# Computing the whole gate half of a gMLP layer by seven block products instead of two thirds of it, in a two-layer trunk on one core

## The chip, the cores and the metric

The program runs on one core of one Trainium2 chip. The metric is the device time of one execution in microseconds (us); lower is better.

## What is computed

The reference is a trunk of two layers on 512 tokens of width 1024, all in float32:

```python
for i in range(DEPTH):
    mod = cond @ ada_w[i] + ada_b[i]                       # six rows of 1024: the adaLN modulation
    sh1, sc1, g1, sh2, sc2, g2 = split(mod, 6)
    h = rms_norm(x, norm_mix[i]) * (1.0 + sc1) + sh1
    y = chunked_relpos_attention(h, ...) if i == 0 else chunked_spatial_gating(h, ...)
    x = x + g1 * y
    h = rms_norm(x, norm_ffn[i]) * (1.0 + sc2) + sh2
    x = x + g2 * (square(relu(h @ w1)) @ w2)               # hidden width 4096

def chunked_spatial_gating(h, w_in, v_gain, w_s, b_s, w_out):
    u, v = split(gelu(h @ w_in), 2)                        # w_in is 1024 x 6144: u and v have 3072 columns
    v = rms_norm(v, v_gain)                                # over all 3072 columns of a token
    vm = mix_positions(v, w_s masked, b_s)                 # windows of 128 tokens
    return (u * vm) @ w_out
```

The change concerns `h @ w_in` for the v half (the gate half) in layer 1: a product of 512 x 1024 by 1024 x 3072.

## The kernel before, in words

**Products.** TensorE (PE) gets float32 operands as pairs: `Split` (L481) makes a rounded high part with a ScalarE cast (L487) and a low part with a VectorE subtract (L488). Every product of two tiles is three matmuls, hi by hi, hi by lo and lo by hi (`mm3`, L92).

**Places.** All large tiles live in 49 places of 4 KB per partition, which `Slots` (L36) hands out from one queue in the order in which they were given back. Whoever takes a place waits for its last user.

**Seven block products.** `seven` (L615) multiplies a 512 x 1024 left operand by a 1024 x 1024 right operand as 2 x 2 blocks of 512, with seven block products in place of eight. Each is done in two half-steps of 256 rows, 12 matmuls each: 168 matmuls for two column blocks of 512. The sums of right operands are made in their places: `plus` is a VectorE add (L632), `grow` a load from HBM that adds to what lies there, issued on GpSimd's queue (L629), and L662 the same from one place to another. A `Step` has four parts: load, right (sums and split of the right operand), left (`prep`, sums and split of the left operand) and mult. `Run.tick` (L724) does a load 7 steps ahead of a mult, and the two splits 3 steps ahead. `Kept` (L561) holds the split left operands of the normed h of layer 1, numbered 0 to 6 by product, for all uses in that layer. Products 0 and 1 use blocks of h itself; product 2 uses the difference of its two lower blocks (token tiles 2 and 3), made by L538.

**The gate half.** Its 3072 columns are six blocks of 512. Block 0 is done plainly by `gate_tile` (four token tiles of 24 matmuls), block 1 plainly by `gate_steps` (four steps of 24 matmuls), and blocks 2 to 5 as two pairs by `seven` with `own=(5, 6)`: the sums for products 5 and 6 are VectorE adds. `Gate.put` collects the results: the first product that reaches a tile is copied from PSUM (L1461), the next is added (L1464), then Gelu (L1465) and the square with its sum (L1467) follow, and each finished pair of tiles is stored to HBM as `vd` (L1438) and loaded again in the mixing. The plain blocks take Gelu straight from PSUM (L1483, L1485).

**Where it starts.** The end of the feed-forward of layer 0 (`project_last`) finishes the residual x tile by tile; `norm.rows(t)` normalizes token tile t and `norm.cols(t)` transposes it (L368) and modulates it on the way out of PSUM (L371, eight ScalarE instructions). The last tile is transposed only after 48 matmuls of the gate half have been issued, so that its norm is hidden. In this region PE follows the written order; elsewhere the scheduler orders each engine.

**Background.** The adaLN rows are worked off piece by piece (`bg`): a load of 512 KB (L179) and a VectorE multiply-add (L194) each, from a queue of 90 that `keep[0]` holds back until later stages.

## Time and profile before

| | |
|---|---|
| median of 3 runs | 1392.52 us (1390.43 to 1395.06) |
| the profiled execution | 1389.62 us, of it 1387.8 us from the first to the last instruction |
| PE busy | 1365.1 us, 98% of the span |
| VectorE (DVE), ScalarE (ACT) busy | 985.6 us, 742.3 us |
| granted TensorE clock | 0.997 of full speed (mean) |

How to read it: the feed-forward of layer 0 runs from 367 us to about 640 us, the gate half from there to about 778 us, and mixing, output product and the second feed-forward follow. The other engines' busy time lies beside PE's unless PE waits; their idle time costs nothing by itself.

### The profile page before, as it was taken

What the parts mean: (1) busy time and instruction counts of PE and PEld (TensorE: products, weight loads), DVE (VectorE), ACT (ScalarE), POOL (GpSimd) and SP (SyncE); (2) the same over time, 40 slices, a digit from 0 to 9 for tenths busy, and PEclk for the clock granted to TensorE, in tenths of its full rate; (3) what the DMA queues carried; (4) which work ended last, traced back from release to release, by engine and by line L of the source; (5) the groups of instructions that cost most, each with busy time, mean ns of one, the idle gap of its engine ahead of it and who ended that gap; (6) DMA issues with size and microseconds to landing.
All of it is one profiled execution on the core that took longest, in us unless ns stands there. A gap on an engine that the chain in (4) does not pass through costs nothing.

```text
span 1387.8 us, 18908 instructions
## 1 busy us (share of the span) xinstructions
PE 1365.1 (98%) x7130; PEld 1168.0 (84%) x7130; DVE 985.6 (71%) x1430; ACT 742.3 (53%) x1249; POOL 83.5 (6%) x98
## 2 busy tenths in 40 slices
PE   8999999999999999999999999999999999999998
PEld 7899888789888888888888888888889988888887
DVE  6889999685657776677796786778855445665672
ACT  6537667665454545537576644466435454554530
POOL 0000000001101102000000001000000110100100
PEclk9999999999999999999999999999999999999999
DMA  9756576574667776458446748575447376655541
GB/s 372 244 138 211 157 209 174 175 286 125 160 187 178 183 226 122 137 183 309 132 165 198 211 152 243 157 193 196 136 136 244 76 155 194 136 155 134 107 152 61
DMA packets 97483, 246.68 MB, mean 178 GB/s; under 512 B 8680, under 2 KB 10096, under 8 KB 97392
## 3 DMA queue, kind: packets, MB, share of 16 engines
q1 hardware_dynamic: 79536, 205.62, 44.6%
q0 software_dynamic: 16128, 33.56, 14.6%
q10 hardware_dynamic: 1728, 6.29, 1.2%
q8 instruction: 56, 0.92, 0.3%
q14 instruction: 35, 0.29, 0.1%
HBM read 219.23 MB, written 14.68 MB: 169 GB/s over the span
## 4 chain that ended last, share of the span: by engine, by line
PE 86%; DVE 6%; DMA 4%; issue 2%; ACT 2%; SPq 0%; POOL 0%; DVEq 0%; ACTq 0%; POOLq 0%
PE p L92 83%; DMA s<-in_a_w_in 1%; DMA s<-xsg 1%; DMA s<-in_ada_w 1%; PE p L1633 1%; DVE s L1222 1%; DVE s L1265 0%; PE p L1260 0%; DMA s<-vd 0%; ACT s L487 0%; DMA s<-s 0%; PE p L207 0%; PE p L317 0%; DVE s L427 0%; DVE s L194 0%
## 5 line engine op out<-in xcount | busy, mean ns | idle before, releaser
L92 PE MATMUL p<-s,s 128*128 128x512 f32 (+2 forms) x6496 | 1302.5, 360 | 9.6 <-DVE nm L1222 2.9
L92 PEld LDWEIGHTS p<-s,s 128*128 128x128 f32 x6496 | 1094.4, 189 | 192.2 <-DVE nm L1222 4.6
L488 DVE TENSOR_TENSOR s<-s,s 128x1024 fp32r<-128x1024 f32 x308 | 371.0, 1223 | 217.6 <-ACT s L487 157.6
L487 ACT CAST s<-s 128x1024 fp32r<-128x1024 f32 x308 | 316.3, 1051 | 195.1 <-PE p L92 106.5
L769 ACT ACTIVATE r<-p 128x512 f32<-128x512 f32 x64 | 38.2, 597 | 123.1 <-PE p L92 121.4
L194 DVE SCALAR_TENSOR_TENSOR s<-s,cs,s 128x1024 f32<-128x1024 f32 x70 | 89.7, 1281 | 12.3 <-DMA s<-in_ada_w 11.7
L629 POOL DMA_DIRECT2D s<-in_ffn_w x48 | 58.3, 1215 | 496.0 <-DVE s L488 408.9
L525 DVE TENSOR_TENSOR s<-s,p 128x512 f32<-128x512 f32 x76 | 50.3, 683 | 15.5 <-PE p L92 15.2
L390 ACT CAST s<-s 128x1024 fp32r<-128x1024 f32 x36 | 37.4, 1051 | 37.8 <-DMA s<-in_ffn_w 14.9
L391 DVE TENSOR_TENSOR s<-s,s 128x1024 fp32r<-128x1024 f32 x36 | 43.4, 1222 | 10.3 <-ACT s L390 10.1
L775 ACT ACTIVATE s<-r 128x256 f32<-128x256 f32 (+1 forms) x112 | 44.9, 442 | 1.4
L426 DVE TENSOR_TENSOR tr<-p,s 128x512 f32<-128x512 f32 (+1 forms) x33 | 22.0, 672 | 31.6 <-PE p L92 31.3
L538 DVE TENSOR_TENSOR s<-s,s 128x1024 f32<-128x1024 f32 x28 | 33.6, 1223 | 10.9 <-PE p L92 10.5
L1227 ACT ACTIVATE s<-s,nm 128x128 f32<-128x128 f32 (+3 forms) x64 | 36.0, 564 | 7.8 <-DVE nm L1222 6.4
L632 DVE TENSOR_TENSOR s<-s,s 128x1024 f32<-128x1024 f32 x28 | 34.0, 1224 | 4.9 <-DMA s<-in_b_w_in 4.7
L321 ACT ACTIVATE tt<-p,mod,mod 128x128 f32<-128x128 f32 x64 | 24.0, 462 | 21.0 <-PE p L317 7.7
L427 DVE TENSOR_TENSOR s<-s,tr 128x512 f32<-128x512 f32 (+1 forms) x33 | 22.1, 675 | 15.0 <-DMA s<-xsg 14.4
L304 ACT ACTIVATE s<-s 128x512 f32<-128x512 f32 x24 | 15.3, 636 | 32.6 <-DVE s L427 30.3
L1265 DVE TENSOR_TENSOR s<-p,s 128x512 fp32r<-128x512 f32 (+3 forms) x64 | 29.3, 486 | 2.8 <-ACT s L1264 2.4
L1222 DVE CUSTOM_DVE_ANT_0 s<-p,s 128x128 f32<-128x128 f32 (+3 forms) x64 | 29.6, 486 | 1.9 <-PE p L92 1.7
L1637 ACT COPY s<-p 128x512 f32<-128x512 f32 x24 | 13.8, 583 | 26.8 <-PE p L1633 26.8
L1264 ACT CAST s<-p 128x512 fp32r<-128x512 f32 (+3 forms) x64 | 25.0, 427 | 5.5 <-PE p L1260 4.4
(149 smaller groups left out, 769.5 us busy)
## 6 DMA issues: line engine op xcount, KB each, us to landing
s<-in_ffn_w SPq DMA_DIRECT2D x116, 512.0 KB, 4.3
s<-in_ada_w SPq DMA_DIRECT2D x96, 512.0 KB, 5.4
s<-in_ffn_w POOLq DMA_DIRECT2D x48, 512.0 KB, 5.8
s<-in_b_w_in SPq DMA_DIRECT2D x48, 512.0 KB, 4.5
s<-in_b_w_out SPq DMA_DIRECT2D x24, 512.0 KB, 4.3
s<-in_a_w_in SPq DMA_DIRECT2D x22, 512.0 KB, 5.0
s<-s SPq DMA_DIRECT2D x64, 128.0 KB, 4.4
vd<-s ACTq DMA_DIRECT2D x12, 512.0 KB, 3.8
```

Source lines behind the costliest of these rows:

```text
L92: T.matmul(ps, lhsT, rhs, start=start, stop=stop, skip_group_check=more)
L194: V.scalar_tensor_tensor(acc, r, ck, acc, ALU.mult, ALU.add)
L390: A.copy(hi, raw)
L391: engs[len(ids) // 2 % len(engs)].tensor_tensor(lo, raw, f32(hi), ALU.subtract)
L487: A.copy(self.hi, raw)
L488: mark[0] = V.tensor_tensor(self.lo, raw, f32(self.hi), ALU.subtract)
L525: V.tensor_tensor(dst, dst, ps, op)
L629: G.dma_start(raw[name, s_][0], block(i, j, s_), accum_op=ALU.add)
L769: A.activation(r, ps, AF.Relu)
L775: A.activation(d, v, AF.Square)
L1222: V.tensor_tensor_reduce(out=pt[it], in0=ps[:, 0:n], in1=b["bias"][:, 512 - n:512], scale=-1.0, scalar=-NEG, op0=ALU.add, op1=ALU.min, acc ...
L1227: last_of["exp"] = A.activation(pt[it], pt[it], AF.Exp, bias=nm[:, it:it + 1], scale=-1.0, accum_out=sm[:, it:it + 1])
```

## The change

- The gate half has three pairs of blocks, and all three go by `seven`. `gate_tile`, `gate_steps`, `gate_end` and `gate_load` are gone. The plan runs the first two pairs interleaved: products 0 and 1 of the first pair, products 0 and 1 of the second, product 2 of both, and then the rest one after the other.
- `own` is now `()`: the right operands of products 5 and 6 are made by adding transfers on GpSimd's queue in place of VectorE adds. For the first two pairs `far` is set: the sum for product 2 is made by an adding load right after product 0's split, and its VectorE add is dropped.
- `Kept.first` makes left operands 0 and 1 (from tokens 0 to 255); `prep` makes the others, operand 6 among them, which was made early before.
- In place of the load for block 0, the first seven ticks (loads and splits) run in `project_last`; eight ticks with a mult (96 matmuls) follow, with `norm.cols(3)` and the preparation of left operand 2 in their middle.
- A tick does its left part before its right part.
- Places that a store gives back (`xs0`, `xsg`, `vd`) go to a queue of their own, `stored`, and are handed first to tiles that a load fills.
- The feed-forward of layer 0 does four background pieces where it did three (nine times), and 27 rather than 36 are held back.

The diff, most unchanged lines left out, with the removed plain functions cut:

```diff
@@ -36,17 +36,25 @@
         self.pool, self.prefix = pool, prefix
-        self.q = deque(range(n))
+        self.q = deque((0, i) for i in range(n))
+        self.stored = deque()
         self.n = 0
-    def get(self, shape, dtype):
-        i = self.q.popleft()
+    def get(self, shape, dtype, load=False):
+        q, s = self.q, self.stored
+        if s and (not q or s[0][0] + (0 if load else 16) < q[0][0]):
+            q = s
+        i = q.popleft()[1]
         self.n += 1
     def free(self, *ids):
-        self.q.extend(ids)
+        self.q.extend((self.n, i) for i in ids)
+    def free_stored(self, *ids):
+        self.stored.extend((self.n, i) for i in ids)
 @with_exitstack
...
@@ -561,17 +569,14 @@
     class Kept(Spent):
-        def half(self, i):
+        def first(self):
             for j in range(2):
-                self.op[((0, 1), ("r", 6))[i][j]] = Split(self.ab[i, j][0], [P, 4, 256])
-        def rows(self):
-            return plain({(0, 0): self.op[0], (0, 1): self.op[1], (1, 0): self.op.get("r"), (1, 1): self.op.get(6)})
+                self.op[j] = Split(self.ab[0, j][0], [P, 4, 256])
         def prep(self, m):
-            if m in self.op:
+            if m in self.op or m < 2:
                 return
                 2: (("x", (1, 0), (1, 1), ALU.subtract),),
@@ -579,8 +584,8 @@
                 5: (((0, 0), (0, 0), (1, 0), ALU.subtract),),
                 self.comb(*c)
-            self.op[m] = Split(self.ab[("x", "x", (0, 1), (0, 0))[m - 2]][0], [P, 4, 256])
-            self.spend(*((), ("x",), ((0, 1),), ((0, 0), (1, 0), (1, 1)))[m - 2])
+            self.op[m] = Split(self.ab[("x", "x", (0, 1), (0, 0), (1, 1))[m - 2]][0], [P, 4, 256])
+            self.spend(*((), ("x",), ((0, 1),), ((0, 0), (1, 0)), ((1, 1),))[m - 2])
             if d not in self.ab:
@@ -612,7 +617,8 @@
-    def seven(left, src, y, own=None):
+    def seven(left, src, y, own=None, far=False):
         raw, op, ps = {}, {}, {}
@@ -622,7 +628,7 @@
             return src[r0:r0 + 256, j * 512:j * 512 + 512].rearrange("(k p) n -> p k n", p=P)
         def load(name, i, j, s_):
-            raw[name, s_] = t, n = SL.get([P, 2, 512], F32)
+            raw[name, s_] = t, n = SL.get([P, 2, 512], F32, True)
             SP.dma_start(t, block(i, j, s_))
         def grow(i, j, name, s_):
@@ -644,7 +650,7 @@
                     grow(*add, name, s_)
             name = {0: "x", 1: "z", 2: "x", 4: "y", 3: "x", 5: "w", 6: "z"}[m]
-            if m == 2:
+            if m == 2 and not far:
                 plus("x", "w", s_)
                 plus(*{5: ("w", "y"), 6: ("z", "x")}[m], s_)
@@ -652,7 +658,9 @@
             late = m in (5, 6) and m not in own and waited[0] is not None
                 op[m, s_] = Split(raw[name, s_][0], [P, 2, 512])
-            if m == 2 and 5 not in own:
+            if m == 0 and far:
+                grow(0, 1, "x", s_)
+            elif m == 2 and 5 not in own:
                 grow(1, 1, "w", s_)
                 plus("x", "y", s_)
@@ -724,7 +732,7 @@
         def tick(self):
             self.i += 1
-            for j, part in ((i + self.ll + self.lp, "load"), (i + self.lp, "right"), (i + self.lp, "left"), (i, "mult")):
+            for j, part in ((i + self.ll + self.lp, "load"), (i + self.lp, "left"), (i + self.lp, "right"), (i, "mult")):
                 if 0 <= j < n:
@@ -846,7 +854,7 @@
             if hf == 0:
                     SP.dma_start(xs[t], xt[t])
-                    SL.free(xid[t])
+                    SL.free_stored(xid[t])
         any_order()
         up_done(1)
@@ -1436,10 +1444,10 @@
         A.dma_start(vd[cb, b], v.rearrange("p t n -> p (t n)"))
-        SL.free(i)
+        SL.free_stored(i)
...
@@ -1458,79 +1466,18 @@
             dst = vv[cb, t // 2][0][:, t % 2, :]
                 self.seen.add((t, hf))
-                A.copy(dst, ps)
+                waited[0] = A.copy(dst, ps)
                 return
             tt = tp.tile([P, 512], F32, tag="tt", name="vq")
-            A.activation(tt, dst, AF.Square, accum_out=vss[:, t, cb:cb + 1])
+            waited[0] = A.activation(tt, dst, AF.Square, accum_out=vss[:, t, cb:cb + 1])
             if t % 2:
-    def gate_tile(cb, t, w):
...
-    steps = gate_steps(1)
-    for p in (1, 2):
-        steps += seven(kept, b_w_in[0][:, SGH + p * 1024:SGH + (p + 1) * 1024], Gate(p), (5, 6))
+    pre = [seven(kept, b_w_in[0][:, SGH + p * 1024:SGH + (p + 1) * 1024], Gate(p), (), p < 2) for p in range(3)]
+    steps = pre[0][:4] + pre[1][:4] + pre[0][4:6] + pre[1][4:6] + pre[0][6:] + pre[1][6:] + pre[2]
     bsT = cp.tile([P, SGG], F32, name="bsT")
...
@@ -1712,7 +1658,7 @@
             for n in range(8)
-    steps[3].mult = then(steps[3].mult, mixing)
+    pre[0][-1].mult = then(pre[0][-1].mult, mixing)
     steps[-1].mult = then(steps[-1].mult, row_scales)
         ahead[0] = wload(b_w_out[0][2048:3072, 0:512], KD)
@@ -1740,28 +1686,26 @@
         norm.rows(t)
             with tc.issue_after(normed[0].ins):
-                kept.half(0)
-    lead[0], keep[0] = 2, 36
-    ffn(0, mid, gate_rows, norm.cols, lambda: gate_load(0), [3] * 9, 2, last_of["o"])
+                kept.first()
+    run = Run(steps, 4, 3)
+    lead[0], keep[0] = 2, 27
+    ffn(0, mid, gate_rows, norm.cols, lambda: [run.tick() for _ in range(7)], [4] * 9, 2, last_of["o"])
+    ahead.clear()
     close(0, 5)
         SP.dma_start(xs[t], xt[t])
-        SL.free(xid[t])
-    keep[0] = 27
-    ws = [ahead.pop("w")]
-    for t in range(2):
-        gate_tile(0, t, ws[0][0])
+        SL.free_stored(xid[t])
+    for i in range(4):
+        with tc.issue_after(normed[0].ins) if i > 1 else nullcontext():
+            run.tick()
     norm.cols(NT - 1)
-    kept.half(1)
-    run = Run(steps, 4, 3)
+    kept.prep(2)
     with tc.issue_after(normed[0].ins):
-        run.prime()
-    for t in range(2, NT):
-        gate_tile(0, t, ws[0][0])
+        for _ in range(4):
+            run.tick()
     any_order()
-    SL.free(*ws[0][1])
     keep[0] = 9
```

What the programs' instruction lists show: matmuls of 128x512 go from 4614 to 4590, ACT casts of 128x1024 from 370 to 375, ACT copies of 128x512 from 122 to 128, DVE operations of 128x1024 (two tensors) from 446 to 443 and of 128x512 from 254 to 260, and GpSimd's transfers from 64 to 80 (10 of the 16 more from HBM, 6 from place to place). The attention layer's order does not change.

DVE at the first norm (token tile 0), before; `p` is the last product of the feed-forward, L426 and L427 add its gated result to x, L130 to L137 make the row scale and L308 the normed tile:

```order
L391 TENSOR_TENSOR s17_681_6130<-s9_679_6127,s43_680_6129 128x1024 [waits DMAHW3_49,Activation_49]
L426 TENSOR_TENSOR tr_6192<-p7_284_6167,s26_435_4480 128x512 [waits PE_49]
L427 TENSOR_TENSOR s16_415_4341<-s16_415_4341,tr_6192 128x512 [waits DVE_49]
L130 TENSOR_SCALAR ra_6203<-ss_6200 128x1 [waits Activation_49]
L133 SCALAR_TENSOR_TENSOR ru_6205<-ry_6204,ra_6203 128x1 [waits Activation_49]
L137 SCALAR_TENSOR_TENSOR ru_6205<-ru_6205,ry_6204 128x1 [waits DVE_49]
L308 TENSOR_SCALAR s36_689_6199<-s16_415_4341,ru_6205 128x1024 [waits DVE_49]
```

And in the change (every line is eight higher):

```order
L496 TENSOR_TENSOR s28_695_6173<-s43_687_6157,s14_694_6172 128x1024 [waits DMAHW1_49,Activation_49]
L496 TENSOR_TENSOR s29_692_6166<-s12_686_6155,s42_691_6165 128x1024 [waits DMAHW2_49,Activation_49]
L434 TENSOR_TENSOR tr_6236<-p4_286_6211,s17_435_4480 128x512 [waits PE_49]
L435 TENSOR_TENSOR s11_417_4347<-s11_417_4347,tr_6236 128x512 [waits DVE_49]
L138 TENSOR_SCALAR ra_6247<-ss_6244 128x1 [waits Activation_49]
L496 TENSOR_TENSOR s0_698_6180<-s26_688_6159,s25_697_6179 128x1024 [waits DMAHW5_49,Activation_49]
L141 SCALAR_TENSOR_TENSOR ru_6249<-ry_6248,ra_6247 128x1 [waits Activation_49]
L145 SCALAR_TENSOR_TENSOR ru_6249<-ru_6249,ry_6248 128x1 [waits DVE_49]
L316 TENSOR_SCALAR s7_703_6243<-s11_417_4347,ru_6249 128x1024 [waits DVE_49]
```

Three subtracts of right operands of the gate half have come between the last product of tile 0 and its norm, two of them ahead of the add, one behind the mean; each waits for a cast, and those casts wait for loads. In the same way two subtracts and a multiply stand ahead of the norm of token tile 2, where before there were none.

ACT around the last modulation (`norm.cols(3)`: L371 before, L379 in the change), before; `s` are places, `p` banks of PSUM, `vd` the stored gate half, and a wait on DMAHW or DMASW is for a transfer of SP's or ACT's, or of GpSimd's queue:

```order
L1483 ACT_TABLE_LOAD
L1483 ACTIVATE s27_700_6494<-p5_297_6495 128x512 [waits PE_49]
L1485 ACTIVATE vq_6529,vss_3643<-s27_700_6494 128x512 [waits Activation_49]
L1483 ACTIVATE s27_700_6494<-p4_298_6531 128x512 [waits PE_49]
L1485 ACTIVATE vq_6560,vss_3643<-s27_700_6494 128x512 [waits Activation_49]
L1438 DMA vd_3642<-s27_700_6494 128x1024 [waits DMAHW5_49]
L371 ACTIVATE s42_687_6197<-p7_299_6563,mod10_5676,mod11_5101 128x128 [waits PE_49]
L371 ACTIVATE s42_687_6197<-p7_299_6563,mod10_5676,mod11_5101 128x128 x3
L371 ACTIVATE s6_688_6198<-p6_300_6572,mod10_5676,mod11_5101 128x128 [waits PE_49]
L371 ACTIVATE s6_688_6198<-p6_300_6572,mod10_5676,mod11_5101 128x128 x3
L487 CAST s7_735_6752<-s39_717_6603 128x1024 [waits DMAHW1_49,DVE_49]
L487 CAST s11_739_6785<-s5_720_6609 128x1024 [waits DMAHW4_49,DMAHW2_49,DVE_49]
```

In the change, from the last instruction of the modulation on:

```order
L495 CAST s0_742_6742<-s34_693_6170 128x1024 [waits DMASW7_49]
L495 CAST s35_749_6788<-s11_737_6694 128x1024 [waits DMAHW0_49,PE_49,Activation_49]
L1469 COPY s42_736_6685<-p0_305_6658 128x512 [waits PE_49]
L1473 ACT_TABLE_LOAD
L1473 ACTIVATE s20_720_6571<-s20_720_6571 128x512 [waits DVE_49]
L1469 COPY s42_736_6685<-p7_306_6665 128x512 [waits PE_49]
L1473 ACTIVATE s20_720_6571<-s20_720_6571 128x512 [waits DVE_49]
L1475 ACTIVATE vq_6615,vss_3643<-s20_720_6571 128x512 [waits Activation_49]
L1475 ACTIVATE vq_6625,vss_3643<-s20_720_6571 128x512 [waits Activation_49]
L1446 DMA vd_3642<-s20_720_6571 128x1024
L495 CAST s15_753_6812<-s12_686_6155 128x1024 [waits DVE_49,PE_49]
L495 CAST s18_728_6648<-s21_727_6646 128x1024 [waits DVE_49]
```

The Gelu tables (ACT_TABLE_LOAD) were loaded before the modulation and are now loaded behind it; between the modulation and the cast of left operand 2 (`s18_728`) stand eleven more instructions, of which the first waits for a transfer on GpSimd's queue. Its lo part is made by DVE behind that cast.

DVE behind the last norm, before; `cs` is the condition of the background pieces (L194):

```order
L488 TENSOR_TENSOR s18_707_6582<-s42_687_6197,s25_706_6581 128x1024 [waits Activation_49]
L488 TENSOR_TENSOR s10_732_6720<-s0_714_6597,s41_731_6719 128x1024 [waits DMAHW3_49,Activation_49]
L194 SCALAR_TENSOR_TENSOR s19_704_6526<-s37_725_6672,cs_79,s19_704_6526 128x1024 [waits DMAHW6_49,DVE_49]
L632 TENSOR_TENSOR s0_714_6597<-s0_714_6597,s48_730_6717 128x1024 [waits DVE_49]
L488 TENSOR_TENSOR s1_709_6586<-s6_688_6198,s35_708_6585 128x1024 [waits Activation_49]
L194 SCALAR_TENSOR_TENSOR s19_704_6526<-s31_729_6714,cs_79,s19_704_6526 128x1024 [waits DVE_49]
```

And in the change, up to the lo part of left operand 2 (`s9_729`); L1472 adds a product's result to the gate half, L638 is `plus`, L546 makes the difference for left operand 2:

```order
L1472 TENSOR_TENSOR s20_720_6571<-s20_720_6571,p4_301_6587 128x512 [waits PE_49]
L1472 TENSOR_TENSOR s20_720_6571<-s20_720_6571,p2_302_6594 128x512 [waits PE_49]
L638 TENSOR_TENSOR s12_686_6155<-s12_686_6155,s2_733_6672 128x1024 [waits DVE_49]
L638 TENSOR_TENSOR s43_687_6157<-s43_687_6157,s11_737_6694 128x1024 [waits DMAHW0_49,DVE_49]
L546 TENSOR_TENSOR s21_727_6646<-s46_701_6241,s39_702_6242 128x1024 [waits Activation_49]
L496 TENSOR_TENSOR s40_743_6743<-s34_693_6170,s0_742_6742 128x1024 [waits DMASW7_49,Activation_49]
L496 TENSOR_TENSOR s31_750_6789<-s11_737_6694,s35_749_6788 128x1024 [waits Activation_49]
L496 TENSOR_TENSOR s19_754_6813<-s12_686_6155,s15_753_6812 128x1024 [waits Activation_49]
L1472 TENSOR_TENSOR s42_736_6685<-s42_736_6685,p4_307_6701 128x512 [waits PE_49]
L496 TENSOR_TENSOR s9_729_6649<-s21_727_6646,s18_728_6648 128x1024 [waits Activation_49]
```

Seven subtracts stand between the last norm and the first of these rows. The background pieces that stood here are gone into the feed-forward; the adds of `Gate.put`, two sums of right operands and the difference for left operand 2 have come, and the lo part stands last. On GpSimd's queue eight adding loads (L635) come in between the feed-forward and the mixing, where there were none; the last, into `s34_693`, waits for the first subtract behind the last norm, and the first ACT row of the change above waits for it. On PE, 48 matmuls stand between the transposes of `norm.cols(3)` and the first use of left operand 2; its hi part is used alone for six matmuls, and the seventh needs the lo part.

## Rows read from the trace of the kernel before

**Rows 1.** The page's first part: busy time of each engine, its share of the span and its number of instructions; and the head of its chain of work that ended last, by engine.

```profile
PE 1365.1 (98%) x7130; PEld 1168.0 (84%) x7130; DVE 985.6 (71%) x1430; ACT 742.3 (53%) x1249; POOL 83.5 (6%) x98
...
PE 86%; DVE 6%; DMA 4%; issue 2%; ACT 2%; SPq 0%; POOL 0%; DVEq 0%; ACTq 0%; POOLq 0%
```

**Rows 2.** Busy time of each engine by stretch (us from the span's start), with instructions, then the granted clock, the busy share of the DMA engines and GB/s: the feed-forward of layer 0, its last product, the plain blocks of the gate half, its other blocks.

```profile
367.00:607.00 240.00, 240.00 (x1069) 198.93 (x1068) 162.15 (x163) 119.70 (x162) 22.86 (x19) 1.00 0.67 179
607.00:652.00 45.00, 45.00 (x214) 37.50 (x212) 30.44 (x45) 22.80 (x53) 0.00 (x0) 1.00 0.68 247
652.00:711.00 59.00, 59.00 (x269) 48.90 (x268) 49.68 (x47) 38.10 (x65) 0.61 (x2) 1.00 0.53 177
711.00:778.00 67.00, 67.00 (x298) 55.46 (x297) 47.56 (x47) 45.48 (x75) 4.17 (x4) 1.00 0.63 193
```

**Rows 3.** PE's timeline: start, length, line, operation and count. L368 are the transposes of `norm.cols`.

```profile
613.27 1.03 PE L368 MATMUL p<-ident,s 128*128 128x128 f32 x8
...
636.84 1.03 PE L368 MATMUL p<-ident,s 128*128 128x128 f32 x8
637.62 14.32 PE L92 MATMUL p<-s,s 128*128 128x512 f32 x62
651.78 1.03 PE L368 MATMUL p<-ident,s 128*128 128x128 f32 x8
652.57 32.47 PE L92 MATMUL p<-s,s 128*128 128x512 f32 x142
```

**Rows 4.** DVE's timeline at the norms of token tiles 0 and 2, in the same form; in brackets idle time and what ended it.

```profile
609.77 0.21 DVE L130 TENSOR_SCALAR ra<-ss 128x1 f32<-128x1 f32 x1 [0.79 <-ACT s L304]
...
610.70 0.75 DVE L308 TENSOR_SCALAR s<-s,ru 128x1024 f32<-128x1024 f32 x1
...
631.22 0.22 DVE L130 TENSOR_SCALAR ra<-ss 128x1 f32<-128x1 f32 x1 [0.93 <-ACT s L304]
...
632.15 0.76 DVE L308 TENSOR_SCALAR s<-s,ru 128x1024 f32<-128x1024 f32 x1
```

**Rows 5.** ACT's timeline at a cast of the plain blocks' right operand and around the last norm, in the same form; in brackets idle time and what ended it.

```profile
603.76 1.05 ACT L390 CAST s<-s 128x1024 fp32r<-128x1024 f32 x1 [5.08 <-DMA s<-in_b_w_in]
...
647.78 1.28 ACT L1483 ACT_TABLE_LOAD   x1
649.07 0.60 ACT L1483 ACTIVATE s<-p 128x512 f32<-128x512 f32 x1
649.70 0.63 ACT L1485 ACTIVATE vq<-s 128x512 f32<-128x512 f32 x1
...
652.78 2.89 ACT L371 ACTIVATE s<-p,mod,mod 128x128 f32<-128x128 f32 x8
655.52 5.83 ACT L487 CAST s<-s 128x1024 fp32r<-128x1024 f32 x6
672.15 0.60 ACT L1483 ACTIVATE s<-p 128x512 f32<-128x512 f32 x1 [10.80 <-PE p L92]
```

**Rows 6.** DVE's timeline there: L308 is the last norm.

```profile
648.24 0.75 DVE L308 TENSOR_SCALAR s<-s,ru 128x1024 f32<-128x1024 f32 x1
648.91 3.49 DVE L488 TENSOR_TENSOR s<-s,s 128x1024 fp32r<-128x1024 f32 x3
652.32 3.92 DVE L194 SCALAR_TENSOR_TENSOR s<-s,cs,s 128x1024 f32<-128x1024 f32 x3
```

**Rows 7.** Groups of instructions by line and shape, of DVE from 367 to 1010 us and of ACT from 560 to 780 us: count, busy us and mean ns of one, idle time before them and what ended it.

```profile
L632 DVE TENSOR_TENSOR s<-s,s 128x1024 f32<-128x1024 f32 x28 | 34.0, 1224 | 4.9 <-DMA s<-in_b_w_in 4.7
L538 DVE TENSOR_TENSOR s<-s,s 128x1024 f32<-128x1024 f32 x12 | 14.4, 1222 | 4.8 <-PE p L92 4.8
L1464 DVE TENSOR_TENSOR s<-s,p 128x512 f32<-128x512 f32 x12 | 8.1, 686 | 1.7 <-PE p L92 1.7
...
L1461 ACT COPY s<-p 128x512 f32<-128x512 f32 x12 | 6.9, 586 | 2.4 <-PE p L92 1.6 <-DMA vd<-s 0.7
```

**Rows 8.** The page's part on DMA issues: out<-in, issuing queue and count, KB each, median us from issue to landing; the third row is of 607 to 660 us alone.

```profile
s<-in_ffn_w POOLq DMA_DIRECT2D x48, 512.0 KB, 5.8
s<-in_b_w_in POOLq DMA_DIRECT2D x6, 512.0 KB, 8.5
s<-in_b_w_in SPq DMA_DIRECT2D x11, 512.0 KB, 8.2
vd<-s ACTq DMA_DIRECT2D x12, 512.0 KB, 3.8
```

**Rows 9.** All adding loads from HBM (L629): the least, median and greatest time from issue to landing; GpSimd's timeline with two of them in the gate half; then rows of SP's timeline, two loads of the gate half's weights and a store of x.

```profile
DMA to landing us min/median/max: 5.6/6.0/10.4
...
754.77 1.21 POOL L629 DMA_DIRECT2D s<-in_b_w_in  x1 [71.98 <-DMA s<-in_b_w_in]
757.55 1.20 POOL L629 DMA_DIRECT2D s<-in_b_w_in  x1 [1.58 <-DVE s L632]
...
599.05 0.94 SPq L387 DMA_DIRECT2D s<-in_b_w_in  x2
...
630.32 0.33 SPq L1750 DMA_DIRECT2D xsg<-s  x1
```

**Rows 10.** The page's DMA queues: packets, MB, and the time of the packets as a share of 16 engines' span.

```profile
q1 hardware_dynamic: 79536, 205.62, 44.6%
q0 software_dynamic: 16128, 33.56, 14.6%
```

More of the change, by code (lines that the diff above doesn't have):

```diff
@@ L130, in rsqrt_m2 @@
             V.tensor_scalar(a, ss, ss2, EPS, ALU.add, ALU.add)
-        A.activation(y, a, AF.Abs_reciprocal_sqrt)
+        rooted[0] = A.activation(y, a, AF.Abs_reciprocal_sqrt)
         if w == 1:
@@ L155, in raw_tile @@
     def raw_tile(shape):
-        t, i = SL.get(shape, F32)
+        t, i = SL.get(shape, F32, True)
         return t, lambda: SL.free(i)
@@ L295, in split_of @@
         return [(tiles[k // 2][0][:, k % 2, :], tiles[k // 2][1][:, k % 2, :]) for k in range(2 * len(tiles))]
-    normed, squared = [None], [None]
+    normed, squared, rooted = [None], [None], [None]
     def norm_rows(t, eng=V):
@@ L1466, in put @@
             tt = tp.tile([P, 512], F32, tag="tt", name="vq")
-            A.activation(tt, dst, AF.Square, accum_out=vss[:, t, cb:cb + 1])
+            waited[0] = A.activation(tt, dst, AF.Square, accum_out=vss[:, t, cb:cb + 1])
             if t % 2:
                 v_store(cb, t // 2)
-    def gate_tile(cb, t, w):
-        if (cb, t // 2) not in vv:
-            vv[cb, t // 2] = SL.get([P, 2, 512], F32)
-        ps, pi = bank()
-        gemm_tok(kept.rows(), w, t, ps)
-        bg(1)
-        gate_end(cb, t, ps)
-        PS.free(pi)
@@ L1559, in mixing @@
         PS.free(pi)
-        kept.op.pop("r").free()
     def row_scales():
@@ L1675, in load @@
             hf, j, o = n // 4, 1 - n // 2 % 2, n % 2
-            t, i = raw[n] = SL.get([P, 2, 512], F32)
+            t, i = raw[n] = SL.get([P, 2, 512], F32, True)
             r0 = p * 1024 + j * 512 + o * 256
```

46 lines of the change are left out of this document (2 added, 44 removed).

## The prediction

> **What bounds the kernel now.** I read the page's busy times first: PE is busy 98% of the span and carries 86% of the chain that ended last [rows 1]. Then the stretches: from 367 to 778 us PE has no idle time that shows, with DVE at 68% to 84% of the time and ACT at 50% to 68%, and the full clock [rows 2]. So a matmul that goes away is worth its whole length, and anything else counts only where PE has to wait for it. Then I read PE's timeline for the pace and for the moments at which PE needs something [rows 3], and DVE's and ACT's for how long before those moments it was ready [rows 4 to 6]. The reader is to see there three places: the transposes of token tile 0 at 613.27 us, those of tile 2 at 636.84, and the first matmuls that use tokens 256 to 511, 48 matmuls behind the transposes of tile 3 at 651.78.
>
> A measurement of this kernel can tell about 0.3% from no change, 4.2 us.
>
> **The gain.** Two plain blocks are 2 x 96 = 192 matmuls, a pair by seven products is 168, so 24 go. 62 matmuls took 14.16 us from 637.62 to 651.78 [rows 3], 0.228 us each, so **-5.5 us**. That is all there is to win: PE had hardly any idle time in this stretch.
>
> **The first use of left operand 2.** Before, what stands 48 matmuls behind the transposes of tile 3 needs a cast of the modulated block, and ACT had it done in time and was then idle for 10.80 us [rows 5]. Now it needs the difference of two blocks, its cast and its subtract, behind work that has come in on both engines. PE wants the hi part at 652.57 + 48 x 0.228 = 663.5 us, and, six matmuls later, the lo part at 664.9.
>
> By DVE: the last norm begins at 648.24 and the next instruction at 648.91 [rows 6]. From there the change has seven subtracts at 3.49 / 3 = 1.16 us (657.1), two adds of a product at 0.69 (658.4), two sums at 1.22 (660.9), the difference at 1.22 (662.1), three more subtracts at 1.22 (665.8), an add (666.5) and the lo part (667.7) [rows 6, 7]. That is 2.8 us late.
>
> By ACT: the modulation ends at 655.52 [rows 5], and the first cast then waits for the last adding load. That load is issued when the first subtract has ended, at 650.1; the 48 in the feed-forward, where the DMA engines are as busy as here (0.67 and 0.68 [rows 2]), took 5.8 us in the median [rows 8], so it lands at 655.9. Two casts at 0.97 (657.9), a copy that waits for 24 matmuls, until 658.1 (658.7), the tables at 1.28 (660.0), Gelu, copy, Gelu at 0.6 (661.8), two squares at 0.63 (663.0) and two casts (665.0) [rows 5, 7]; then DVE's third subtract, which needs the first of these casts, the add and the lo part at 667.1, 2.2 us late.
>
> I take **+2.5 us**, between the two, since the DVE route hangs on where the last norm ends. The ends: 0, if DVE and ACT come to this place 2.8 us earlier than before; and with an adding load of 8.5 us [rows 8] or of 10.4, the slowest one [rows 9], 4.9 or 6.8 late.
>
> ACT's table load took 1.28 us and the next instruction began 1.29 us after its start, at 649.07 [rows 5]; no drain shows. The Trainium skill (ScalarE: Activation LUTs, "What ACT_TABLE_LOAD costs") counts 2.66 us for a switch, 1.38 of it a drain. By that the ACT route would end 1.4 us later and the sum would come out about 0.8 us higher; the trace of this kernel speaks for the shorter time.
>
> **The first norms.** Three subtracts come in ahead of the norm of tile 0. Before, it was ready at 610.70 + 0.75 = 611.45, 1.8 us before its transposes [rows 3, 4]. The subtract between mean and scale and the cast that it waits for cost about 1.4 of this; the other two are hidden if their loads have landed. That leaves 0.4 us. For tile 2 two subtracts and a multiply, 2 x 1.22 + 0.69 = 3.1 us, come ahead of a norm that was ready at 632.91, 3.9 us early: 0.8 is left. Nothing is lost at either if each row holds to 0.4 us. But the loads are those whose counterpart made ACT wait 5.08 us before [rows 5], and they are issued behind each other: at the 8.2 us that such a load took in the busy stretch [rows 8] in place of 4.7 (issued at 599.05 [rows 9], cast at 603.76), tile 0 would be 3.5 - 0.4 = 3.1 us late. I take **+0.5 us**, nearer the lower end, since the DMA engines are idle for a third of that time [rows 2]; ends 0 and 3.1.
>
> **What costs nothing.** Nine background pieces move into the feed-forward: a DVE instruction of 3.92 / 3 = 1.31 us each [rows 6], 11.8 us in 240 us where DVE is idle for 78 [rows 2]; without that cover they would cost at most these 11.8. Five casts at 0.97, six copies and six adds at 0.59 and 0.69, less three adds at 1.22 [rows 5, 7], are 8.4 us on ACT and 0.5 on DVE, beside a PE that has 126 us of work there while ACT is idle for 42 [rows 2]. Sixteen more transfers on GpSimd's queue: 64 took 14.6% of the span, 3.17 us each [rows 10], 51 us more. From 607 to 778 the DMA engines were busy 0.68 x 45 + 0.53 x 59 + 0.63 x 67 = 104 us of 171 [rows 2]; with 51 more it is 0.90, and less what the nine background loads took, which leave (44.6% of the span for 205.62 MB, so 1.6 us each [rows 10]), 0.82. Not full, but loads will land later. Where places go to loads behind a store, the load waits for the store: 3.8 us for `vd` [rows 8], within a lead of seven steps, 84 x 0.228 = 19 us. From the mixing on PE's order is the old one, and I count nothing.
>
> **The sum.** -5.5 + 2.5 + 0.5 = -2.5 us. The profiled execution took 1389.62 us, so it would take 1387.1; the median of the runs is 2.9 above that execution, so I forecast **1390.0 us**.
>
> **The rivals.**
>
> A, operand 2 is ready in time: the full gain, 1392.5 - 5.5 = **1387.0 us**, faster. For it: DVE stood idle 0.93 and 0.79 us at the norms [rows 4], and a last norm 2.8 us earlier is enough. Against it: the seven subtracts all stand behind that norm, whatever is ready earlier.
>
> B, slower: the adding loads do not overlap. Eight now stand on a queue that was empty here. If each begins only when the one ahead has landed, then the five last ones, which cannot begin before their base loads (issued behind the store at 630.32 [rows 9], landed about 636, an estimate from 4.7 and queuing) end at 636 + 5 x 5.8 = 665.0 in place of 655.9. ACT's first cast waits 9 us, operand 2 comes 11.1 us late, and the sum is -5.5 + 11.1 + 0.5 = +6.1, **1398.6 us**. From 4.5 us a load upwards it takes the whole gain. Against it: two adding loads were issued at 754.77 and 757.55 [rows 9], 2.8 us apart, and such loads took 5.6 us at the least [rows 9]; GpSimd did not wait for the first to land before it issued the second. The Trainium skill (DMA: Bandwidth & Descriptors, "Anatomy of one DMA — SWDGE (gpsimd) path") fits 2.0 us and the bytes over 436 KB per us to such a transfer, 3.2 us for 512 KB; by that B would end near 652 and cost nothing. The 5.8 us of the trace are against that figure.
>
> C, a norm waits for loads: tile 0 or tile 2 is late by the upper end, -5.5 + 2.5 + 3.1 = +0.1, **1392.6 us**, no change. For it: covers of 0.4 and 0.8 us, and DMA busier than before.
>
> That the change would not do what it says is no rival: the matmuls are counted.
>
> **How the numbers follow.** The forecast 0.48, A 0.25, C 0.17, B 0.10. Faster by over 0.3% (under 1388.3): nearly all of A and the low edge of the forecast, 0.27. Slower (over 1396.7): B less its milder part, and the worst of C, 0.10. Within: 0.63. The range goes from A less the spread of medians, 1386.2, to C with operand 2 at its 4.9, 1395.0; it leaves out B and the tails, about 0.15.
>
> **What would show it.** Right: 24 matmuls of 128x512 fewer; PE idle for 2 to 3 us near 664 us, with the subtract or the cast of operand 2 as releaser; the transposes at 613, 637 and 652 us within 1 us of their places; the distance from there to the mixing 3 us shorter. For A, no idle time of PE at 664. For B, a wait of several us of ACT for an adding load ahead of the tables. For C, PE idle ahead of a group of transposes. The prediction is wrong at its root if PE is idle by more than 1 us elsewhere between 660 and 780, which the cover of seven steps is to prevent, or if the feed-forward is longer, which nine background pieces would then have caused.

## The result: slower by 0.41%, 5.5 us of matmuls saved and 11 us of waits and slow clock added

The changed kernel took 1398.13 us in the median of 6 runs (1395.63 to 1399.69), the kernel before 1391.55 in 6 runs on the same chip: **ratio 1.0041, 95% interval 1.0028 to 1.0055** (it is not the quotient of the two medians, which is 1.0047 and lies inside the interval). The forecast was 1390.0 with a range to 1395.0 and 0.10 for slower. The profiled execution of the change took 1395.63 us, 1393.9 of it from the first to the last instruction, 6.1 more than before.

The head of its page, with the chain of work that ended last by engine; it answers to [rows 1].

```profile
PE 1363.0 (98%) x7106; PEld 1165.2 (84%) x7106; DVE 985.7 (71%) x1433; ACT 750.1 (54%) x1260; POOL 100.7 (7%) x114
...
PE 83%; DMA 6%; DVE 5%; ACT 3%; issue 2%; SPq 0%; POOL 0%; DVEq 0%; POOLq 0%; ACTq 0%
```

PE has 24 instructions fewer, as counted, but its part of the chain fell from 86% to 83%, and that of DMA rose from 4% to 6%. The stretches of [rows 2], in the same columns, and a last one of 3.9 us:

```profile
367.00:607.00 240.00, 240.00 (x1068) 198.75 (x1068) 167.82 (x169) 117.22 (x160) 23.15 (x20) 1.00 0.70 192
607.00:652.00 45.00, 44.15 (x207) 36.31 (x206) 30.03 (x45) 26.45 (x56) 7.54 (x7) 1.00 0.81 227
652.00:711.00 59.00, 52.63 (x233) 43.21 (x232) 43.52 (x42) 40.09 (x65) 6.42 (x8) 0.94 0.69 178
711.00:778.00 67.00, 67.00 (x296) 54.94 (x295) 45.48 (x46) 47.23 (x78) 8.40 (x8) 1.00 0.85 235
672.10:676.00 3.90, 3.90 (x10) 3.12 (x11) 3.90 (x6) 3.49 (x7) 0.00 (x0) 0.53 0.00 0
```

The feed-forward is as it was, PE without idle time. The loss sits between 652 and 711 us: 6.4 us idle, and a granted clock of 0.94. PE's timeline there, which answers to [rows 3], and its transposes in the second feed-forward (L325):

```profile
615.47 1.06 PE L376 MATMUL p<-ident,s 128*128 128x128 f32 x8 [0.85 <-DVE s L316]
...
653.79 1.03 PE L376 MATMUL p<-ident,s 128*128 128x128 f32 x8
654.58 11.14 PE L100 MATMUL p<-s,s 128*128 128x512 f32 x48
672.09 27.64 PE L100 MATMUL p<-s,s 128*128 128x512 f32 x113 [6.37 <-ACT s L495]
...
1035.50 1.06 PE L325 MATMUL p<-ident,s 128*128 128x128 f32 x8 [1.21 <-DVE s L316]
1048.44 1.06 PE L325 MATMUL p<-ident,s 128*128 128x128 f32 x8 [0.94 <-DVE s L316]
1064.97 1.06 PE L325 MATMUL p<-ident,s 128*128 128x128 f32 x8 [1.19 <-DVE s L316]
```

The transposes of the second feed-forward that waited in the kernel before (L317 there):

```profile
1043.14 1.06 PE L317 MATMUL p<-ident,s 128*128 128x128 f32 x8 [0.59 <-DVE s L308]
1058.90 1.06 PE L317 MATMUL p<-ident,s 128*128 128x128 f32 x8 [0.43 <-DVE s L308]
```

So the 6.1 us come together, against before, but for smaller terms: 24 matmuls, -5.5. The first use of left operand 2, 48 matmuls behind the last transposes as expected, waits 6.37 for a cast on ACT. Behind this gap the clock is at 0.53, near the lower of its two levels (1.2 of 2.4 GHz), and ten matmuls take 3.90 us; the 113 of that row took 27.64, at 0.228 each they would take 25.8: 1.9. Token tile 0: 0.85. The second feed-forward's norms: 3.34, where the same transposes waited 0.59 and 0.43 before, so 2.3. Sum: **+5.9**. That this is so near 6.1 is in part chance: two waits in the mixing, 0.22 and 0.49 us before, are gone, so that 0.9 of the 6.1 us stand in no wait and no slow stretch that the profile shows.

What ACT did ahead of that cast; it answers to [rows 5]. L379 is the last modulation, L1469 the copy of a product from PSUM, L1473 Gelu.

```profile
655.41 1.05 ACT L495 CAST s<-s 128x1024 fp32r<-128x1024 f32 x1 [5.46 <-DMA s<-in_b_w_in]
656.37 2.89 ACT L379 ACTIVATE s<-p,mod,mod 128x128 f32<-128x128 f32 x8
663.51 2.00 ACT L495 CAST s<-s 128x1024 fp32r<-128x1024 f32 x2 [4.25 <-DMA s<-in_b_w_in]
665.41 0.57 ACT L1469 COPY s<-p 128x512 f32<-128x512 f32 x1
666.00 1.28 ACT L1473 ACT_TABLE_LOAD   x1
667.30 0.63 ACT L1473 ACTIVATE s<-s 128x512 f32<-128x512 f32 x1
...
670.05 2.93 ACT L495 CAST s<-s 128x1024 fp32r<-128x1024 f32 x3
```

No instruction of ACT overtakes another here: the copy at 665.41 starts 11.6 us behind the last transposes, and in op2_hard (below), where no waiting cast stands ahead of it, 5.2 us behind them. Twice ACT stands before a cast of a right operand whose load has not landed. The first is a plain load into `s2_733`, issued at 643.29 and landed at 655.38; the modulation behind it starts at 656.37, 2.6 us behind the start of its transposes, where it was 1.0 before [rows 3, 5]. The second is the adding load into `s34_693`, issued at 652.73 and landed at 663.48, 10.75 us. Only then come copy, table load, Gelu and squares, and left operand 2's cast among the three at 670.05; PE goes on at 672.09. DVE was not the last here: it had the difference for operand 2 at 663.3 and then waited for ACT.

Why the loads were late shows in the DMA engines from 636 to 664 us: their busy share in 40 slices of 0.7 us (9 is 90% or more), the two queues' packets, MB and share, and the adding loads' count, KB and median us to landing.

```profile
DMA  9999987889999999999999999999999999999399
...
q0 software_dynamic: 1693, 3.40, 66.7%
q1 hardware_dynamic: 1654, 3.64, 36.4%
...
s<-in_b_w_in POOLq DMA_DIRECT2D x6, 512.0 KB, 10.5
```

The same stretch before, which had no transfer on q0:

```profile
DMA  9999999999999999999999999998999410278700
...
q1 hardware_dynamic: 4095, 8.60, 83.2%
```

In the change the engines are full for nearly all of these 28 us. GpSimd's queue (q0) holds them for 0.667 x 28 = 18.7 us to move 3.40 MB: 2.9 us for a load of 0.52 MB. The plain loads on q1 take 0.364 x 28 / 3.64 x 0.52 = 1.5 us. Before, q1 moved 8.60 MB with 83.2%, 1.4 us for a load. Over the whole span of the change q0 took 17.6% of the engines' time for its 80 transfers, 41.95 MB, 3.1 us each, so the price does not hang on this stretch. The Trainium skill (Trainium Kernel Development and Optimization, "Key Constraints") says that transfers issued from SP, ACT and GpSimd run on the same 16 DMA engines and that issuing from several saves only issue time. On the sharing the trace agrees: the engines are full, and the two queues' shares add up to 103%; what issuing from several queues saves, no run here shows.

### The profile page after: what moved, and what is told of

The parts are those of the page before. It is cut to its first block, busy times and chain, and to the rows that moved or that the text cites. A ratio compares the mean times of both kernels' runs of the same rounds, so it can differ in the third digit from the quotient of the medians.

```text
span 1393.9 us, 18927 instructions
## 1 busy us (share of the span) xinstructions
PE 1363.0 (98%) x7106; PEld 1165.2 (84%) x7106; DVE 985.7 (71%) x1433; ACT 750.1 (54%) x1260; POOL 100.7 (7%) x114
## 3 DMA queue, kind: packets, MB, share of 16 engines
q0 software_dynamic: 19712, 41.95, 17.6%
## 4 chain that ended last, share of the span: by engine, by line
PE 83%; DMA 6%; DVE 5%; ACT 3%; issue 2%; SPq 0%; POOL 0%; DVEq 0%; POOLq 0%; ACTq 0%
PE p L100 80%; DMA s<-in_ada_w 2%; DMA s<-in_b_w_in 1%; DMA s<-xsg 1%; ACT s L495 1%; DMA s<-in_a_w_in 1%; PE p L1579 1%; PE p L1268 1%; DVE s L496 1%; DVE s L399 1%; DMA s<-in_ffn_w 0%; DMA s<-in_x 0%; DVE s L1230 0%; DVE s L991 0%; DVE s L1273 0%
## 5 line engine op out<-in xcount | busy, mean ns | idle before, releaser
L496 DVE TENSOR_TENSOR s<-s,s 128x1024 fp32r<-128x1024 f32 x317 | 380.4, 1222 | 218.3 <-ACT s L495 147.4
L495 ACT CAST s<-s 128x1024 fp32r<-128x1024 f32 x317 | 326.6, 1050 | 229.0 <-PE p L100 101.0
L635 POOL DMA_DIRECT2D s<-in_ffn_w x48 | 57.9, 1209 | 501.4 <-DVE s L496 451.9
L398 ACT CAST s<-s 128x1024 fp32r<-128x1024 f32 x32 | 33.2, 1052 | 30.5 <-DMA s<-in_ffn_w 18.4
L399 DVE TENSOR_TENSOR s<-s,s 128x1024 fp32r<-128x1024 f32 x32 | 38.5, 1221 | 10.3 <-ACT s L398 10.1
L546 DVE TENSOR_TENSOR s<-s,s 128x1024 f32<-128x1024 f32 x28 | 33.6, 1222 | 6.0 <-PE p L100 3.8
L635 POOL DMA_DIRECT2D s<-in_b_w_in x16 | 19.5, 1243 | 252.5 <-ACT s L495 71.5
L638 DVE TENSOR_TENSOR s<-s,s 128x1024 f32<-128x1024 f32 x20 | 24.3, 1221 | 9.6 <-DMA s<-in_b_w_in 9.6
```

Of the source, the lines that this page charges most:

```text
L398: A.copy(hi, raw)
L399: engs[len(ids) // 2 % len(engs)].tensor_tensor(lo, raw, f32(hi), ALU.subtract)
L495: A.copy(self.hi, raw)
L496: mark[0] = V.tensor_tensor(self.lo, raw, f32(self.hi), ALU.subtract)
L546: V.tensor_tensor(self.ab[d][0], self.ab[a][0], self.ab[b][0], o)
L635: G.dma_start(raw[name, s_][0], block(i, j, s_), accum_op=ALU.add)
```

## The experiments

Four theories stood for the late operand 2: **T**, an adding load holds the DMA engines about twice as long as a plain one; **Q**, GpSimd's queue itself is slow; **P**, places handed out behind stores make loads start late; **O**, the order of the work on DVE and ACT. **S** concerns the second feed-forward, where a weight load is now issued just ahead of the adding load of the residual; **D** says that DVE becomes the bound. All ratios are to the kernel before on the same chip; the runs stood on more than one chip, so ratios are to be compared between rows, not medians. Each edit is against the changed kernel. The last two columns are PE's idle time in one profiled execution, at the first use of left operand 2 and ahead of the four groups of transposes of the second feed-forward.

| run | median us | ratio, 95% interval | PE idle at operand 2's first use, us | L325 idle, us |
|---|---|---|---|---|
| the change | 1398.13 | 1.0041, 1.0028 to 1.0055 | 6.4 | 3.3 |
| plain_write | 1390.87 | 1.0009, 0.9994 to 1.0025 | 0.8 | 3.6 |
| far_off | 1397.09 | 1.0051, 1.0032 to 1.0070 | 1.5, then 4.5 from 706 to 720 | 4.9 |
| far_first | 1400.85 | 1.0079, 1.0060 to 1.0099 | 2.8 | 3.6 |
| one_queue | 1397.10 | 1.0049, 1.0034 to 1.0064 | 5.3 | 1.2 |
| late_free | 1396.64 | 1.0032, 1.0019 to 1.0045 | 6.7 | 1.3 |
| own_all | 1395.77 | 1.0031, 1.0018 to 1.0044 | 3.6 | 3.7 |
| own_01 | 1396.76 | 1.0042, 1.0027 to 1.0057 | 3.4 | 4.2 |
| own_all_l | 1394.88 | 1.0027, 1.0014 to 1.0039 | 3.8 | 1.0 |
| op2_hard | 1390.40 | 0.9997, 0.9985 to 1.0009 | 0, then 0.95 | 3.3 |
| op2_hard_l | 1388.48 | 0.9978, 0.9966 to 0.9990 | 0, then 0.95 | 1.7 |
| op2_hard_own_l | 1397.79 | 1.0043, 1.0030 to 1.0056 | 0, then 4.9 at 677 to 688 | 1.1 |

### plain_write: the same transfers without the adding

```diff
-            G.dma_start(raw[name, s_][0], block(i, j, s_), accum_op=ALU.add)
+            if own is None:
+                G.dma_start(raw[name, s_][0], block(i, j, s_), accum_op=ALU.add)
+            else:
+                G.dma_start(raw[name, s_][0], block(i, j, s_))
```

> Leaves out the adding: GpSimd's transfers of right operands from HBM in the gate half and the mixing write the block in place of adding it (the sums there are wrong); number, queue, bytes loaded and order of instructions stay as in the change. Theory T (an adding load keeps the DMA engines busy twice as long as a plain one, 2.9 against 1.5 us of all 16 for 512 KB, so they are full from 636 to 664 us and ACT's casts ahead of left operand 2 wait for them): the transfers land 4 to 9 us after their issue in place of 8 to 14, ACT waits less than 1 us for one ahead of the tables, PE is idle 1 to 3.5 us at the first use of operand 2 in place of 6.4, and the time is 1391 to 1394 us. Theory Q (GpSimd's queue itself is slow): landings stay at 8 to 14 us and the idle time above 5. Theory P (places: the loads are issued too late because they wait for stores): idle time above 5, time 1396 to 1399.

What this kernel computes is wrong by the missing sums; it is there for its time alone. Its PE at the first use of operand 2, and the DMA engines from 636 to 664 us:

```profile
665.37 1.19 PE L100 MATMUL p<-s,s 128*128 128x512 f32 x4 [0.16 <-ACT s L495]
666.79 0.73 PE L100 MATMUL p<-s,s 128*128 128x512 f32 x2 [0.23 <-DVE s L1475]
667.93 24.55 PE L100 MATMUL p<-s,s 128*128 128x512 f32 x107 [0.40 <-DVE s L496]
```

```profile
q0 software_dynamic: 952, 3.51, 38.9%
q1 hardware_dynamic: 1582, 3.40, 33.2%
...
s<-in_b_w_in POOLq DMA_DIRECT2D x6, 512.0 KB, 6.8
```

On the same queue, into the same places, 3.51 MB now hold the engines for 10.9 us, 1.6 for a load, and the loads land in 6.8 us in the median, the slowest in 7.3. The idle time at operand 2 falls from 6.4 to 0.8 us and the ratio from 1.0041 to 1.0009; the intervals don't meet. T holds; Q and P, which leave this run as slow as the change, do not. Idle time and median lie just below what T had named (1 to 3.5 us, 1391 to 1394). Even so the kernel is only as fast as before: the norms of the second feed-forward still wait 3.6 us.

### far_off and far_first: fewer early adding loads

```diff
-    pre = [seven(..., Gate(p), (), p < 2) for p in range(3)]
+    pre = [seven(..., Gate(p), (), False) for p in range(3)]    # far_off; far_first has p < 1
```

> far is off for both pairs: the four adding loads that made product 2's sums are gone, DVE adds two loaded blocks instead (four more of 1.22 us). T: the DMA engines are done with their backlog some 6 us earlier, no cast of ACT ahead of operand 2 waits for GpSimd's queue, PE idle at operand 2 is 1.5 to 4 us (DVE has more to do ahead of it), time 1391 to 1395 us. P: idle above 5, 1396 to 1399. Theory O (only the order of DVE's and ACT's work ahead of operand 2 matters): idle grows by up to 4.9 us, 1399 to 1404.

> far stays on for the first pair alone: two adding loads fewer, among them the one that ACT's first cast behind the modulation waited for. T: PE idle at operand 2 is 1.5 to 4 us, time 1391 to 1395 us. P: above 5, 1396 to 1399. O: idle grows by up to 2.4 us.

In far_off operand 2 is nearly in time, but three waits come in its place between 706 and 720 us, 4.5 us in all. The longest:

```profile
709.02 7.09 PE L100 MATMUL p<-s,s 128*128 128x512 f32 x30 [2.60 <-DVE s L1472]
```

In far_first the cast of `s2_733` slipped ahead of the last norm's root on ACT (L139), and the last transposes themselves came late. Its ACT, and its PE:

```profile
652.69 1.05 ACT L495 CAST s<-s 128x1024 fp32r<-128x1024 f32 x1 [4.53 <-DMA s<-in_b_w_in]
653.65 0.19 ACT L139 ACTIVATE ry<-ra 128x1 f32<-128x1 f32 x1
```

```profile
656.26 1.94 PE L376 MATMUL p<-ident,s 128*128 128x128 f32 x8 [2.53 <-DVE s L316]
```

Neither is faster than the change, and both miss the 1391 to 1395 us that T gave them, though the idle time at operand 2 is as T had it. O by itself fails too: by it the idle time there should have grown. In far_first the late transposes and the late operand together, 2.5 and 2.8 us, cost no more idle time than the operand alone in the change, 6.4; why its ratio is the highest of all stays open. But far_first showed what to test next: a late load is paid for by whatever the scheduler puts behind its cast on ACT.

### one_queue and late_free: the places of stores

one_queue gives all places back to the one queue; late_free does so for the second feed-forward alone.

```diff
     def free_stored(self, *ids):
-        self.stored.extend((self.n, i) for i in ids)
+        self.free(*ids)                                       # one_queue
...
-                    SL.free_stored(xid[t])
+                    (SL.free if l else SL.free_stored)(xid[t])  # late_free
```

> Places that stores give back go to the one common queue again; all else as in the change. P: the loads are issued earlier, PE idle at operand 2 falls below 3.5 us, time 1391 to 1394. T: the same adding loads are in the same stretch, idle stays between 4 and 8 us, time 1395 to 1400 us.

> As the change, but in the second feed-forward the places that the stores of x give back go to the common queue. In the change a weight load that takes such a place is issued at 1019.4 us, just ahead of the adding load of the residual at 1020.7, which lands after 7.1 us (before: 5.2), and PE waits 3.3 us in all for the three norms that hang on these. Theory S (that load delays the adding load): PE's waits ahead of the transposes at 1035, 1048 and 1065 us fall from 3.3 to about 1 us, time 2 to 2.5 us below the change, 1395.5 to 1396.5 us; the wait at left operand 2 stays at 5.5 to 7 us. Rival: the norms are late for another reason, waits stay at 3 us or more, time as the change.

Both keep the stall at operand 2 (5.29 and 6.70 us), so P is not its cause. Both take the waits of the second feed-forward's norms from 3.3 to 1.2 or 1.3 us. Their group in late_free, from 1010 to 1090 us:

```profile
L325 PE MATMUL p<-ident,s 128*128 128x128 f32 x32 | 4.2, 274 | 1.3 <-DVE s L316 1.3
```

The adding load of the residual landed after 5.43 us there, 7.07 in the change, 5.24 before. The table bears S out further: the five runs in which the second feed-forward gives its places to the common queue wait 1.0 to 1.7 us there, the seven others 3.3 to 4.9. So S holds for these 2 us, but its route is traced for the first of the three norms alone, 1.2 us; the other two adding loads took nearly the same in both (5.26 and 9.84 us in the change, 5.28 and 9.66 in late_free). On the time this is too little to show by itself: the interval of late_free overlaps that of the change. In one_queue a new wait of 2.48 us for a subtract on DVE at 786.50 takes back most of what it had gained. late_free's median, 1396.64, lies just above the 1395.5 to 1396.5 that S gave it.

### own_all, own_01, own_all_l: sums on DVE in place of adding transfers

```diff
-    pre = [seven(..., Gate(p), (), p < 2) for p in range(3)]
+    pre = [seven(..., Gate(p), (5, 6), False) for p in range(3)]   # own_01: (5, 6) for the first two pairs
```

own_all_l is own_all with late_free's edit.

> All three pairs of the gate half with own=(5, 6) and far off: every sum of right operands by DVE adds, no adding transfer in the gate half; seven products as in the change, interleaved as in the change. T (adding transfers hold the DMA engines): no wait for GpSimd's queue, PE idle at left operand 2 0.5 to 2 us, the waits of the run without far near 709 and 718 us gone too, time 1390 to 1393. Rival D (DVE becomes the bound when it makes the sums): PE idle in the gate half 4 us or more, time 1395 to 1400.

> As the run with all sums on DVE, but the third pair makes its sums for products 5 and 6 by adding transfers (two adding loads, two from place to place, after 711 us, where the DMA engines have room). T: as that run within 2 us. Should the adding transfers cost wherever they stand: 2 us or more slower than that run, with PE idle between 730 and 780 us.

> Both: all sums of the gate half on DVE, and the common queue for the places of the second feed-forward. T and S together: the gains add, 2 to 2.5 us below the run with all sums on DVE, 1388 to 1391 us, faster than before by up to 3 us. If either is wrong: no less than that run.

No adding transfer is left at operand 2, the DMA engines are busy 0.13 of the time from 645 to 670 us instead of 0.99, and PE still waits. own_all's PE, and that stretch (columns as in [rows 2]):

```profile
665.01 1.20 PE L100 MATMUL p<-s,s 128*128 128x512 f32 x4 [1.04 <-ACT s L495]
668.59 13.50 PE L100 MATMUL p<-s,s 128*128 128x512 f32 x50 [2.38 <-DVE s L1472]
```

```profile
645.00:670.00 25.00, 21.58 (x96) 16.94 (x94) 24.82 (x26) 18.41 (x31) 0.00 (x0) 0.98 0.13 52
```

DVE is busy 24.82 of 25 us: the wait has only moved from the DMA engines to DVE. That is D, for this way out; the median is in D's range (1395 to 1400), and the idle time, 3.6 us, just under its 4. own_01, whose third pair adds by transfers after 711 us, is as slow as own_all within 1 us, so there these transfers cost nothing that shows. own_all_l misses its 1388 to 1391: the second norms wait 1.0 us in place of 3.7, but the median falls by only 0.9 us, and the intervals overlap.

### op2_hard, op2_hard_l, op2_hard_own_l: operand 2 ahead of the casts that wait

The three ticks behind the eight written out by hand, whose casts are those that waited, are tied behind both halves of operand 2, on ACT and on DVE. The transfers stay the same.

```diff
-            A.copy(self.hi, raw)
+            cast[0] = A.copy(self.hi, raw)
...
     kept.prep(2)
+    two = (cast[0].ins, mark[0].ins)
...
     keep[0] = 9
+    with tc.issue_after(two[0]), tc.issue_after(two[1]):
+        for _ in range(3):
+            run.tick()
     run.go()
```

op2_hard_l adds late_free's edit, op2_hard_own_l that and own_all's.

> The change as it is, but the three ticks that follow product 1 (splits for steps 11 to 13) are put behind both halves of left operand 2 on ScalarE and VectorE; loads and adding loads are untouched. Theory T2 (late adding loads cost time only because their casts stand ahead of operand 2 on ScalarE, in order): PE's idle time at the first use of operand 2 falls from 6.4 us to under 1, the slow clock behind it goes (some 1.9 us more), and the median falls by 6 to 8 us to 1390 to 1392. Rival T1 (the transfers themselves are short of what PE needs): the right operand of that product or of the next steps is late instead, PE idles 4 to 6 us there, and the median stays at 1396 to 1399.

> op2_hard, and the stores of the second feed-forward give their places back to the common queue as before. T2 with S (a weight load just ahead of an adding load of the residual makes the second feed-forward's norms late): 1.5 to 2 us less than op2_hard, 1388 to 1390, 2 to 4 us faster than the kernel before. T1: 1395 to 1397.

> op2_hard_l with the sums for products 2, 5 and 6 of all three pairs as VectorE adds, no adding transfer in the gate half. T2: operand 2 no longer behind the sums on VectorE, 1388 to 1391, like op2_hard_l. Rival D (VectorE itself is short of time from 648 to 680 us, where it is busy all through): PE still idles 2 us or more between 660 and 690 and the median is 1392 to 1395.

PE in op2_hard: no idle time from the last transposes for 100 matmuls, with the first use of operand 2 among them, then a small wait for a cast at 679.22. Behind it ACT, in the same run:

```profile
654.54 1.04 PE L376 MATMUL p<-ident,s 128*128 128x128 f32 x8
655.33 22.94 PE L100 MATMUL p<-s,s 128*128 128x512 f32 x100
679.22 15.77 PE L100 MATMUL p<-s,s 128*128 128x512 f32 x67 [0.95 <-ACT s L495]
```

```profile
655.17 2.91 ACT L379 ACTIVATE s<-p,mod,mod 128x128 f32<-128x128 f32 x8 [4.48 <-PE p L376]
659.72 0.59 ACT L1469 COPY s<-p 128x512 f32<-128x512 f32 x1 [1.64 <-PE p L100]
...
664.38 3.89 ACT L495 CAST s<-s 128x1024 fp32r<-128x1024 f32 x4
```

The last adding load is as late as in the change: issued at 653.53, landed at 664.42, 10.89 us. But its cast now stands behind that of operand 2, and at 664.42 it is early enough for the step that uses it, three steps later. The median falls from 1.0041 to 0.9997 of before; the intervals don't meet. T2, as the expectation calls it, holds: the late transfer cost time only through the order behind it. The edit changes that order on ACT and on DVE together; that ACT's decided in the change is read from its trace, where DVE had the difference at 663.3 and the cast came only among the three from 670.05 on. The clock is 1.00 from 664 to 680 us, so the slow matmuls went with the gap.

**op2_hard_l beats both kernels**, the one before by 0.2%: 0.9978 (0.9966 to 0.9990). Its span is 1385.0 us, 2.8 under before and 8.9 under the change. This joins the order and S: 6.4 and 1.9 us back at operand 2, 0.85 at token tile 0 and 1.6 at the second norms, less the 0.95 at the new cast and 0.7 by which this execution was already late at 380 us, are 9.1.

op2_hard_own_l, on the other hand, misses T2's 1388 to 1391, and at 1397.79 it is slower than its rival D's 1392 to 1395 too, though with the idle time that D names. DVE is busy 36.89 of the 40 us from 648 to 688, and PE waits for its results and for casts of them:

```profile
683.27 0.73 PE L100 MATMUL p<-s,s 128*128 128x512 f32 x2 [0.84 <-DVE s L496]
687.81 13.60 PE L100 MATMUL p<-s,s 128*128 128x512 f32 x48 [3.81 <-ACT s L495]
```

So adding transfers are the better place for these sums after all, given the right order behind them.

## Why the prediction was wrong, step by step

**The gain** was right: 24 matmuls fewer, 5.5 us. op2_hard_l shows that it can be had in part: its span is 2.8 us under that of before.

**The first use of left operand 2** was the right place, route and mechanism, with the wrong size: +2.5 was taken, 8.3 was measured (6.4 idle, 1.9 at a slow clock). The failed step is the landing of the last adding load: "the 48 in the feed-forward, where the DMA engines are as busy as here (0.67 and 0.68 [rows 2]), took 5.8 us in the median [rows 8], so it lands at 655.9". It landed at 663.48, after 10.75 us. A mean busy share over 45 us said nothing of the moment: already before, the engines were full from 636 to 655 us, and the change put six adding loads there, each holding them for 2.9 us in place of 1.5. That price was in [rows 10], 3.17 us a transfer, and was used for a mean over 171 us only. That mean was even about right: 0.82 was forecast, and (0.81 x 45 + 0.69 x 59 + 0.85 x 67) / 171 = 0.78 came. Of the ends that were named, 10.4 us of landing gave 6.8 late, and 6.4 came. (The 4.9 and the 6.8 are each some 0.2 too long beside the 11.1 of rival B: the copy's own wait for its 24 matmuls takes that much of a late load. Nothing hangs on it.)

Two more things were missing in that step. The cast of the plain load `s2_733` held up the modulation by 1.6 us, which the prediction's ACT route let end where it did before; here this cost nothing, since ACT then stood idle for 4.25 us, but in far_first the same cast made the last transposes late. And the gap cost clock too: no term had the 1.9 us.

**The first norms**: +0.5 was taken, 0.85 came at tile 0, tile 2 lost nothing, as worked out. ACT waited 9.39 us for a load ahead of tile 0 (5.08 before), but that was over at 605.19, ten us before the transposes. The subtract between mean and scale cost more than the 1.4 us that were taken: from L138 to L316 it was 2.81 us, where it was 0.93 before [rows 4], so 1.9.

**What costs nothing** held for the feed-forward with its nine more background pieces and for the 67 us behind 711. It failed at "From the mixing on PE's order is the old one, and I count nothing": PE's order was the old one, but the new queue of places changed when loads start, and the residual's adding load met a weight load. That cost 2.3 us, and late_free and one_queue give 2.0 and 2.2 of it back.

**The rivals.** The time of B came, 1398.6 against 1398.13, but not its mechanism. GpSimd issued the last two loads from 651.88 on, with the load of 644.05 landing at 658.43, so several were under way at once; what they shared was the 16 engines, where B had them wait for each other on the queue. Its figure for the landing of the last, 665.0, was near the true 663.5, but that was luck: it had 5.8 us for each of five loads in a row, and the runs show 2.9 us of full engines for each of six, with plain loads between them. An estimate by the fit of the Trainium skill (DMA: Bandwidth & Descriptors, "Anatomy of one DMA — SWDGE (gpsimd) path"), 2.0 us and the bytes over 436 KB per us, is 3.2 us for 512 KB. The traces left it by far: 8.3 to 14.4 us for the adding loads here, and 4.5 to 7.3 for plain ones on the same queue in plain_write. A was wrong. C was not what decided.

**Still open**: which part of the change's tick order (left before right) and of the moved background pieces matters was not tried alone; neither was tile 0's wait, which was between 0 and 1.8 us in the runs above.

## What to carry to other kernels

When a transfer moves into a stretch, look at the DMA engines in the slices around it, not at the mean of the stretch, and count what each transfer holds of them: an adding load counted about twice here. A late load costs what stands behind its first consumer on its engine, if nothing there overtakes, as on ACT here; before adding buffers or moving sums, put the operand that PE needs next ahead of casts that wait for loads needed later. And when the rule that hands out buffers changes, look at the loads of later stages too: they can move even where no instruction does.
